# A decoder layer: four z tiles and most gate tiles computed ahead of the token mixers, the gate tiles in pairs by seven half-size products

## The chip, the cores and the metric

The kernel runs on one core of a Trainium2 chip. The metric is device time in microseconds (us), the median of three runs. PE is the matrix engine, PEld its weight loads, DVE the vector engine, ACT the scalar engine, POOL the GpSimd engine, and SP issues most DMA transfers.

## The reference

One layer of a decoder over 512 tokens and 2048 channels, all in float32: a token mixer, a cross-attention into 256 memory tokens, a feed-forward block with a short convolution, and a final norm. The change lies in the mixer. One matrix `w_in` (2048 rows) gives all its projections, among them `z` (1024 columns) and the logits of three gates (3 x 2048 columns):

```python
proj = xn @ w_in
dn_qkv, dn_z, dn_a, dn_b, swa_q, swa_kv, sb_qkv, gates = split_cols(proj, IN_SIZES)
...
o_dn = rmsnorm(o_dn, dn_norm) * silu(dn_z)
gate = sigmoid(gates).reshape(bsz, seq, 3, 2048)
merged = gate[:, :, 0] * (y_dn @ w_br_dn) + gate[:, :, 1] * (y_swa @ w_br_swa) + gate[:, :, 2] * (y_sb @ w_br_sb)
return merged @ w_o
```

`y_dn` comes from a recurrence over chunks (gated DeltaNet), `y_swa` from windowed attention, `y_sb` from stick-breaking attention.

## The kernel before

Activations lie feature-major: a tile is 128 features by 512 tokens. To keep float32 accuracy with the fast matrix format, every operand is split into a rounded part (`hi`, or `wh` of a weight) and the rest (`lo`, `wl`). `dense` (line 138) makes one tile of 128 output columns: for each of the 16 slices k of 128 input rows it issues three matmuls of 512 columns (lines 153 to 155: hi·wh, lo·wh, hi·wl), 48 in all. The weights come by SP in pieces of 1024 rows x 128 columns (512 KB, tile `raw`, three buffers); ACT rounds four slices at a time into `wh` (line 149), DVE subtracts to get `wl` (line 150), and each has four buffers of four slices. While PE works on some slices, ACT and DVE prepare the next.

The stages in order of the program: start (lines 164 to 281: norms, keys and values of the memory, matmuls of 256 columns since there are 256 memory tokens; x split into `hi`, `lo`); DeltaNet (lines 294 to 547: q, k, v of two heads at a time, then a long chain of small operations, between which the dense tiles of the next pair, and at the end the eight `z` tiles, stand on PE); the two attentions (lines 553 to 689, with their own dense tiles between small operations); gates and merge (lines 691 to 715); then `w_o`, cross-attention and feed-forward.

In the merge each of 16 column tiles m has, for each of three branches, one dense gate tile (48 matmuls, line 698), a sigmoid on ACT into `sg` (line 700), then a branch product of 24, 12 or 12 matmuls (line 707), a multiply by `sg` on DVE (710, 713) and a sum on POOL (714).

The order on each engine is made by a scheduler from data dependencies, buffers and priorities (weight loads and splits are given a high one); each engine then runs its list strictly in order and waits on semaphores.

Of the kernel before, what the change touches and what calls it, by code (L numbers as in the profile page):

```python
# [9 lines left out]
F32 = mybir.dt.float32  # L10
# [7 lines left out]
P = 128  # L18
# [40 lines left out]
def decoder_kernel(ctx: ExitStack, tc: tile.TileContext, x, mem, norm_mix, w_in, dn_conv, dn_a_log, dn_dt_bias, dn_norm,  # L59
# [13 lines left out]
    wsp = ctx.enter_context(tc.tile_pool(name="wsp", bufs=4))  # L73
    misc = ctx.enter_context(tc.tile_pool(name="misc", bufs=2))
    psd = ctx.enter_context(tc.tile_pool(name="psd", bufs=2, space=bass.MemoryType.PSUM))
    psum = ctx.enter_context(ExitStack())
    gen = []

# [41 lines left out]
    lo = [None] * KT  # L120

    def split_slot(k):
        hi[k] = main.tile([P, S], F32R, name=f"hi{k}")
        lo[k] = main.tile([P, S], F32R, name=f"lo{k}")
        return hi[k], lo[k]

    def mrg_tile(k):
        return main.tile([P, S], F32, name=f"mrg{k}")
# [9 lines left out]
    def dense(acc, w, r0, nk, col, hs, ls, M=P, share=False):  # L138
        for c0 in range(0, nk, 8):
# [3 lines left out]
            with tc.high_priority(1000000):  # L143
                nc.sync.dma_start(out=raw[:, :kc, :], in_=w[r:r + kc * P, col:col + M].rearrange("(k p) c -> p k c", p=P))
            for s0 in range(0, kc, 4):
                wh = wsp.tile([P, 4, M], F32R, name="wh")
                wl = wsp.tile([P, 4, M], F32R, name="wl")
                with tc.high_priority(1000000):
                    act.copy(wh, raw[:, s0:s0 + 4, :])  # L149
                    (pool if share and s0 else dve).tensor_tensor(wl, raw[:, s0:s0 + 4, :], wh.bitcast(F32), op=ALU.subtract)  # L150
                for j in range(4):
                    k = c0 + s0 + j
# [21 lines left out]
    with region("p_start") as ps:  # L174
        memT = [main.tile([P, S], F32R, name=f"mrg{k}") for k in range(KT)]
# [108 lines left out]

    def conv_silu(dst, acc, c):
# [8 lines left out]
    gen_pool("psg_dn", 3)  # L294
    y = [None] * 16
    with region("p_dn") as dp:
# [90 lines left out]
        for h0 in range(0, DNH, 2):  # L387
# [10 lines left out]
            # decays  # L398
# [15 lines left out]
            # keys  # L414
# [17 lines left out]
            # inverse of the unit lower triangular matrices, transposed: blocks of 8 by substitution, then doubling  # L432
# [40 lines left out]
            # queries and values  # L473
# [15 lines left out]
            # the recurrence over chunks  # L489
# [36 lines left out]
            # output norm  # L526
# [14 lines left out]
        for h in range(DNH):  # L541
            acc = dense_ps()
            dense(acc, w_in, 0, KT, O_Z + h * P, xh, xl)
            sz = misc.tile([P, S], F32, name="m0")
            last = act.activation(sz, acc, AF.Silu)
# [401 lines left out]
```

## Time and profile before

| | |
|---|---|
| median of 3 runs | 2918.39 us (2917.04 to 2918.99) |
| profiled execution: span from first to last instruction | 2917.2 us |
| PE busy | 2867.7 us, 98% |
| PEld, DVE, ACT, POOL busy | 81%, 45%, 36%, 9% |
| mean granted clock of PE | 0.996 |
| read from memory | 266.41 MB, 93 GB/s |

The profile comes from one execution; its span is its own time. Matmuls overlap, so the mean duration of one (392 ns for 512 columns) is not what the next one waits; that is read from start to start. Below, "L153" is line 153 of the kernel before.

### The profile page before, as it was taken

To read this page: it belongs to the slowest core of one execution; us is meant where nothing else is said; L and a number is where in the kernel's file an instruction comes from. 1 tells how busy PE (TensorE), PEld (TensorE's weight loads), DVE (VectorE), ACT (ScalarE), POOL (GpSimd) and SP (SyncE) were. 2 spreads that over 40 slices of the span, in tenths; PEclk is the share of its full clock that TensorE was granted. 3 is DMA by queue.
4 is the path that set the end of the run, shared out by engine and by line. 5 is a ranking of instruction groups with operands and counts; after the bars stand their busy time and mean duration, and the time that the engine had idled before them with its cause. 6 is when DMAs were issued, how large, how long until landed. Compare 5 with 4: busy or idle time off the path is not lost.

```text
span 2917.2 us, 34620 instructions
## 1 busy us (share of the span) xinstructions
PE 2867.7 (98%) x13463; PEld 2365.3 (81%) x13463; DVE 1322.4 (45%) x2305; ACT 1046.6 (36%) x1926; POOL 260.0 (9%) x195
## 2 busy tenths in 40 slices
PE   7999999999999999999999999999999999999998
PEld 7787887877778888888888887788888888888887
DVE  7466576336334223223224344544344434443445
ACT  6444344334443222222224334533223323322333
POOL 2100010100000000000000110201001000000002
PEclk9999999999999999999999999999999999999999
DMA  6322212232223333333334432333333333333333
GB/s 206 103 65 73 56 53 73 64 86 65 73 76 98 94 98 98 94 98 98 94 98 124 118 97 73 91 97 99 95 101 94 99 97 94 101 94 96 99 94 116
DMA packets 469941, 272.84 MB, mean 94 GB/s; under 512 B 11249, under 2 KB 450018, under 8 KB 469138
## 3 DMA queue, kind: packets, MB, share of 16 engines
q1 hardware_dynamic: 468576, 268.60, 32.4%
q8 instruction: 105, 1.72, 0.2%
q0 software_dynamic: 560, 1.79, 0.2%
q14 instruction: 58, 0.48, 0.0%
q10 hardware_dynamic: 642, 0.26, 0.0%
HBM read 266.41 MB, written 4.19 MB: 93 GB/s over the span
## 4 chain that ended last, share of the span: by engine, by line
PE 88%; DVE 3%; ACT 1%; issue 1%; POOL 1%; ACTq 0%; DVEq 0%; POOLq 0%
PE acc L155 21%; PE acc L153 21%; PE acc L154 21%; PE gps L875 4%; PE gps L873 4%; PE gps L874 4%; PE gps L153 2%; PE gps L155 2%; PE gps L154 2%; PE gps L471 1%; PE gps L466 1%; DVE wl L150 1%; PE gps L593 0%; PE gps L686 0%; PE gps L651 0%
## 5 line engine op out<-in xcount | busy, mean ns | idle before, releaser
L153 PE MATMUL acc<-hi,wh 128*128 128x512 f32 x2912 | 1140.8, 392 | 0.7 <-ACT hi L132 0.7
L154 PE MATMUL acc<-lo,wh 128*128 128x512 f32 x2912 | 1141.2, 392 | 0.0
L155 PE MATMUL acc<-hi,wl 128*128 128x512 f32 x2912 | 1141.2, 392 | 0.0
L150 DVE TENSOR_TENSOR wl<-raw,wh 128x512 fp32r<-128x512 f32 x826 | 589.0, 714 | 940.5 <-ACT wh L149 917.9
L149 ACT CAST wh<-raw 128x512 fp32r<-128x512 f32 x840 | 521.7, 622 | 1304.7 <-PE acc L154 1093.0
L155 PEld LDWEIGHTS acc<-hi,wl 128*128 128x128 f32 x2912 | 547.9, 188 | 113.0 <-issue 2.3
L153 PEld LDWEIGHTS acc<-hi,wh 128*128 128x128 f32 x2912 | 547.6, 188 | 113.3 <-issue 1.6
L154 PEld LDWEIGHTS acc<-lo,wh 128*128 128x128 f32 x2912 | 547.8, 188 | 111.6 <-issue 0.9
L868 DVE TENSOR_TENSOR wl<-raw,wh 128x512 fp32r<-128x512 f32 x112 | 77.7, 694 | 165.2 <-ACT wh L867 145.0
L867 ACT CAST wh<-raw 128x512 fp32r<-128x512 f32 x112 | 69.8, 623 | 206.7 <-PE gps L874 171.9
L875 PE MATMUL gps<-wl,mrg 128*128 128x512 f32 x368 | 143.3, 389 | 0.0
L873 PE MATMUL gps<-wh,mrg 128*128 128x512 f32 x368 | 143.2, 389 | 0.0
L874 PE MATMUL gps<-wh,mrg 128*128 128x512 f32 x368 | 143.2, 389 | 0.0
L847 POOL TENSOR_TENSOR u<-u 128x512 f32<-128x512 f32 x32 | 58.3, 1823 | 900.8 <-ACT wh L149 801.2
L714 POOL TENSOR_TENSOR mrg<-mrg,m 128x512 f32<-128x512 f32 x32 | 52.2, 1632 | 641.9 <-DVE m L713 641.9
L843 DVE SCALAR_TENSOR_TENSOR u<-v,ffcw,u 128x511 f32<-128x511 f32 (+1 forms) x128 | 96.1, 751 | 14.6 <-ACT u L839 12.3
L153 PE MATMUL gps<-yh,wh 128*128 128x512 f32 x256 | 99.8, 390 | 0.0
L155 PE MATMUL gps<-yh,wl 128*128 128x512 f32 x256 | 99.7, 389 | 0.0
L154 PE MATMUL gps<-yl,wh 128*128 128x512 f32 x256 | 99.7, 389 | 0.0
L837 DVE TENSOR_TENSOR v<-acc,rstd 128x512 f32<-128x512 f32 x64 | 44.3, 692 | 100.5 <-PE acc L155 100.5
L875 PEld LDWEIGHTS gps<-wl,mrg 128*128 128x128 f32 x368 | 69.1, 188 | 14.4
L874 PEld LDWEIGHTS gps<-wh,mrg 128*128 128x128 f32 x368 | 69.1, 188 | 14.3
(425 smaller groups left out, 2537.0 us busy)
## 6 DMA issues: line engine op xcount, KB each, us to landing
raw<-in_w_in_dram SPq DMA_DIRECT2D x196, 512.0 KB, 3.8
raw<-in_w_up_dram SPq DMA_DIRECT2D x128, 512.0 KB, 4.0
raw<-in_w_down_dram SPq DMA_DIRECT2D x64, 512.0 KB, 3.8
raw<-in_w_o_dram SPq DMA_DIRECT2D x32, 512.0 KB, 4.1
raw<-in_w_xkv_dram SPq DMA_DIRECT2D x16, 512.0 KB, 5.0
raw<-in_w_br_dn_dram SPq DMA_DIRECT2D x16, 512.0 KB, 4.0
xraw<-in_x_dram SPq DMA_DIRECT2D x4, 1024.0 KB, 9.3
raw<-in_w_br_swa_dram SPq DMA_DIRECT2D x16, 256.0 KB, 2.7
```

What stands on the lines that cost most here:

```text
L149: act.copy(wh, raw[:, s0:s0 + 4, :])
L150: (pool if share and s0 else dve).tensor_tensor(wl, raw[:, s0:s0 + 4, :], wh.bitcast(F32), op=ALU.subtract)
L153: pe.matmul(acc, wh[:, j, :], hs[k], start=(k == 0), stop=False)
L154: pe.matmul(acc, wh[:, j, :], ls[k], start=False, stop=False)
L155: pe.matmul(acc, wl[:, j, :], hs[k], start=False, stop=(k == nk - 1))
L843: dve.scalar_tensor_tensor(u[:, sh:S], v[:, 0:S - sh], w, u[:, sh:S], op0=ALU.mult, op1=ALU.add)
L847: pool.tensor_tensor(res[0], res[0], res[1], op=ALU.mult)
L867: act.copy(wh, raw[:, i, :])
L868: dve.tensor_tensor(wl, raw[:, i, :], wh.bitcast(F32), op=ALU.subtract)
L873: pe.matmul(acc, ah[j][:, ts], wh, start=(k == 0), stop=False)
L874: pe.matmul(acc, al[j][:, ts], wh, start=False, stop=False)
L875: pe.matmul(acc, ah[j][:, ts], wl, start=False, stop=(k == 7))
```

## The change

Right after the start stage the new kernel computes four of the eight z tiles (`z_tile`) and writes them to DRAM through POOL's DMA queue. Meanwhile DVE and ACT build four combinations of blocks of x (`sums`, tiles `fb`). Then the gate logits of the column tiles m = 2 to 15 are made in pairs, 21 pairs (7 pairs of m, three gates): rows in two halves of 1024, columns in two tiles of 128, tokens in two halves of 256. Each pair is a 2 x 2 by 2 x 2 block product and is made with seven block products (Strassen's scheme in Winograd's form). One product is eight slices, each with one matmul of 512 columns (wh against hi and lo of 256 tokens, side by side) and one of 256 columns (wl against hi). Sums of weight blocks (`combine`) and of results (`fold`) go to DVE; ACT copies two partial results from one PSUM accumulator into another as a start value (`act.copy(b, a)`, `act.copy(d, b)`). The pair's sigmoid goes to one buffer `g` and by POOL's DMA queue to DRAM. In the DeltaNet stage four z tiles are loaded by SP in place of being computed, and in the merge 42 of 48 gate tiles are. The weight buffers `wh`, `wl` are two of eight slices in place of four of four, in every `dense`. The memory region for the merged tiles is closed and opened again around the new stage.

```diff
--- before.py
+++ after.py
-    wsp = ctx.enter_context(tc.tile_pool(name="wsp", bufs=4))
+    wsp = ctx.enter_context(tc.tile_pool(name="wsp", bufs=2))
     misc = ctx.enter_context(tc.tile_pool(name="misc", bufs=2))
-    psd = ctx.enter_context(tc.tile_pool(name="psd", bufs=2, space=bass.MemoryType.PSUM))
+    dram = ctx.enter_context(tc.tile_pool(name="dram", bufs=1, space=bass.MemoryType.DRAM))
...
+    def open_std(n):
+        nonlocal mrgp, psd
+        psum.close()
+        std.close()
+        mrgp = std.enter_context(tc.tile_pool(name=f"mrgp{n}", bufs=1, reuse_waits="tile"))
+        psd = std.enter_context(tc.tile_pool(name=f"psd{n}", bufs=2, space=bass.MemoryType.PSUM, reuse_waits="tile"))
+    open_std(0)
...
-        hi[k] = main.tile([P, S], F32R, name=f"hi{k}")
-        lo[k] = main.tile([P, S], F32R, name=f"lo{k}")
+        both = main.tile([P, 2, S], F32R, name=f"x{k}")
+        hi[k], lo[k] = both[:, 0, :], both[:, 1, :]
+        xb[k] = both
         return hi[k], lo[k]
...
+            wh = wsp.tile([P, 8, M], F32R, name="wh")
+            wl = wsp.tile([P, 8, M], F32R, name="wl")
             for s0 in range(0, kc, 4):
-                wh = wsp.tile([P, 4, M], F32R, name="wh")
-                wl = wsp.tile([P, 4, M], F32R, name="wl")
+                part = slice(s0, s0 + 4)
                 with tc.high_priority(1000000):
-                    act.copy(wh, raw[:, s0:s0 + 4, :])
-                    (pool if share and s0 else dve).tensor_tensor(wl, raw[:, s0:s0 + 4, :], wh.bitcast(F32), op=ALU.subtract)
-                for j in range(4):
-                    k = c0 + s0 + j
+                    act.copy(wh[:, part, :], raw[:, part, :])
+                    (pool if share and s0 else dve).tensor_tensor(wl[:, part, :], raw[:, part, :], wh[:, part, :].bitcast(F32),
+                                                                  op=ALU.subtract)
+                for j in range(s0, s0 + 4):
+                    k = c0 + j
...
+    def z_tile(h):
+        acc = dense_ps()
+        dense(acc, w_in, 0, KT, O_Z + h * P, xh, xl)
+        sz = misc.tile([P, S], F32, name="m0")
+        return sz, act.activation(sz, acc, AF.Silu)
+    ZE = 4
+    HT = S // 2
+    MP = 2
+    z_d = [None] * ZE
+    gate_d = [[None] * KT for _ in range(3)]
+    psum.close()
+    std.close()
+    gp = std.enter_context(region("p_gate"))
+    psd = psum.enter_context(tc.tile_pool(name="psd_z", bufs=2, space=bass.MemoryType.PSUM, reuse_waits="tile"))
+    fb = [gp.tile([P, 2, 4, HT], F32R, name=f"fb{k}", bufs=1) for k in range(8)]
+    def sums(k):
+        u = gp.tile([P, 2, S], F32, name="sm")
+        for j in range(2):
+            dve.tensor_tensor(u[:, j, :], xh[k + 8 * j].bitcast(F32), xl[k + 8 * j].bitcast(F32), op=ALU.add)
+        b11, b12, b21, b22 = (u[:, j, t * HT:(t + 1) * HT] for j in range(2) for t in range(2))
+        v = gp.tile([P, 4, HT], F32, name="sm")
+        for i, (p_, q_) in enumerate(((b12, b11), (b22, v[:, 0, :]), (b22, b12), (b21, v[:, 1, :]))):
+            dve.tensor_tensor(v[:, i, :], p_, q_, op=ALU.subtract)
+        act.copy(fb[k][:, 0, :, :], v)
+        dve.tensor_tensor(fb[k][:, 1, :, :], v, fb[k][:, 0, :, :].bitcast(F32), op=ALU.subtract)
+    for h in range(ZE):
+        sz, _ = z_tile(h)
+        z_d[h] = dram.tile([P, S], F32, name=f"z{h}")
+        pool.dma_start(out=z_d[h], in_=sz)
+        for k in range(2 * h, 2 * h + 2):
+            sums(k)
+    psum.close()
+    with tc.tile_pool(name="psw", bufs=2, space=bass.MemoryType.PSUM, reuse_waits="tile") as pw:
+        banks = {n: [pw.tile([P, S], F32, name=n) for _ in range(2)] for n in ("sb", "sd")}
+        for n in ("sb", "sd"):
+            for t in banks[n]:
+                pe.matmul(t, xh[0][:, 0:P], xh[0], start=True, stop=True)
+        turn = [0]
+        def moving(form):
+            def of(k):
+                if form < 3:
+                    j, t = ((0, 0), (1, 0), (1, 1))[form]
+                    return xb[k + 8 * j][:, :, t * HT:(t + 1) * HT]
+                return fb[k][:, :, form - 3, :]
+            return of
+        B11, B21, B22, T1, T2, T3, T4 = (moving(i) for i in range(7))
+        def product(acc, w, of, first):
+            n = turn[0] = (turn[0] + 1) % 3
+            if n == 0:
+                wh, wl = (gp.tile([P, 8, P], F32R, name=f"s{n_}", bufs=1) for n_ in ("wh", "wl"))
+            else:
+                wh, wl = (wsp.tile([P, 8, P], F32R, name=n_) for n_ in ("wh", "wl"))
+            with tc.high_priority(1000000):
+                act.copy(wh, w)
+                dve.tensor_tensor(wl, w, wh.bitcast(F32), op=ALU.subtract)
+            av = acc.rearrange("p (h c) -> p h c", h=2)
+            for k in range(8):
+                m = of(k)
+                pe.matmul(av, wh[:, k, :], m, start=(first and k == 0), stop=False, skip_group_check=True)
+                pe.matmul(av[:, 0, :], wl[:, k, :], m[:, 0, :], start=False, stop=(k == 7), skip_group_check=True)
+        def fold(dst, half, other):
+            dve.tensor_tensor(dst, half, other, op=ALU.add)
+        def strassen_pair(w, col, out, straight):
+            quad = []
+            with tc.high_priority(1000000):
+                for i, (h, c) in enumerate(((0, 0), (1, 0), (0, 1), (1, 1))):
+                    r = rawp.tile([P, 8, P], F32, name="raw") if i % 2 else gp.tile([P, 8, P], F32, name="sraw", bufs=3)
+                    nc.sync.dma_start(out=r, in_=w[h * 8 * P:(h + 1) * 8 * P, col + c * P:col + (c + 1) * P]
+                                      .rearrange("(k p) c -> p k c", p=P))
+                    quad.append(r)
+            a11, a12, a21, a22 = quad
+            def combine(x_, y_, op):
+                s_ = gp.tile([P, 8, P], F32, name="sm")
+                with tc.high_priority(1000000):
+                    dve.tensor_tensor(s_, x_, y_, op=op)
+                return s_
+            a, b, c, d = (pw.tile([P, S], F32, name=n) for n in ("sa", "sb", "sc", "sd"))
+            product(a, a11, B11, True)
+            act.copy(b, a)
+            if straight:
+                product(a, a12, B21, False)
+            product(c, combine(a11, a21, ALU.subtract), T3, True)
+            s1 = combine(a21, a22, ALU.add)
+            s2 = combine(s1, a11, ALU.subtract)
+            s7 = misc.tile([P, S], F32, name="sg")
+            act.copy(s7, c)
+            product(b, s2, T2, False)
+            if not straight:
+                product(a, a12, B21, False)
+            act.copy(d, b)
+            la = misc.tile([P, HT], F32, name="m0")
+            act.copy(la, a[:, HT:S])
+            fold(out[:, 0, 0:HT], a[:, 0:HT], la)
+            s4 = combine(a12, s2, ALU.subtract)
+            product(d, s1, T1, False)
+            t = misc.tile([P, S], F32, name="m0")
+            dve.tensor_tensor(t, d, s7, op=ALU.add)
+            fold(out[:, 1, HT:S], t[:, 0:HT], t[:, HT:S])
+            product(b, a22, T4, False)
+            t = misc.tile([P, S], F32, name="m0")
+            dve.tensor_tensor(t, b, s7, op=ALU.add)
+            fold(out[:, 1, 0:HT], t[:, 0:HT], t[:, HT:S])
+            product(d, s4, B22, False)
+            la = misc.tile([P, HT], F32, name="m0")
+            act.copy(la, d[:, HT:S])
+            fold(out[:, 0, HT:S], d[:, 0:HT], la)
+        for m in range(MP, KT, 2):
+            for b_ in range(3):
+                g = gp.tile([P, 2, S], F32, name="g", bufs=1)
+                strassen_pair(w_in, O_G + b_ * D + m * P, g, m == MP and b_ == 0)
+                act.activation(g, g, AF.Sigmoid)
+                gd = dram.tile([P, 2, S], F32, name=f"gate{b_}_{m}")
+                pool.dma_start(out=gd, in_=g)
+                gate_d[b_][m], gate_d[b_][m + 1] = gd[:, 0, :], gd[:, 1, :]
+    open_std(1)
...
-            acc = dense_ps()
-            dense(acc, w_in, 0, KT, O_Z + h * P, xh, xl)
-            sz = misc.tile([P, S], F32, name="m0")
-            last = act.activation(sz, acc, AF.Silu)
+            if h < ZE:
+                sz = misc.tile([P, S], F32, name="sg")
+                nc.sync.dma_start(out=sz, in_=z_d[h])
+            else:
+                sz, last = z_tile(h)
             pool.tensor_tensor(y[h], y[h], sz, op=ALU.mult)
...
-                acc = dense_ps()
-                dense(acc, w_in, 0, KT, O_G + b * D + m * P, xh, xl)
                 sg = misc.tile([P, S], F32, name="sg")
-                last = act.activation(sg, acc, AF.Sigmoid)
+                if m < MP:
+                    acc = dense_ps()
+                    dense(acc, w_in, 0, KT, O_G + b * D + m * P, xh, xl)
+                    last = act.activation(sg, acc, AF.Sigmoid)
+                else:
+                    nc.sync.dma_start(out=sg, in_=gate_d[b][m])
                 if m == 0:
...
-                        wh = wsp.tile([P, S], F32R, name="wh")
-                        wl = wsp.tile([P, S], F32R, name="wl")
+                        if i == 0:
+                            whs, wls = (wsp.tile([P, 2, S], F32R, name=n) for n in ("wh", "wl"))
+                        wh, wl = whs[:, i, :], wls[:, i, :]
```

PE in the merge before (`gps` is the accumulator of a branch product, `acc` that of a gate tile, `yh`, `yl` the branch output, `hi`, `lo` the split x; the numbers are buffers). The end of one branch product and the beginning of the next gate tile:

```order
L153 MATMUL gps_8130<-yh11_7228,wh_8133 128x512
L154 MATMUL gps_8130<-yl11_7229,wh_8133 128x512
L155 MATMUL gps_8130<-yh11_7228,wl_8134 128x512
L153 MATMUL acc_8152<-hi0_497,wh_8155 128x512
L154 MATMUL acc_8152<-lo0_498,wh_8155 128x512
L155 MATMUL acc_8152<-hi0_497,wl_8156 128x512
```

PE at the like place now (column tile 3, from the first branch to the second):

```order
L168 MATMUL gps_11385<-yh7_10769,wh_11388 128x512
L169 MATMUL gps_11385<-yl7_10770,wh_11388 128x512
L170 MATMUL gps_11385<-yh7_10769,wl_11389 128x512
L168 MATMUL gps_11422<-yh8_10875,wh_11425 128x512
L169 MATMUL gps_11422<-yl8_10876,wh_11425 128x512
L170 MATMUL gps_11422<-yh8_10875,wl_11426 128x512
```

The 48 matmuls of a gate tile between two branch products are gone for column tiles 2 to 15.

PE in the new stage, between two block products of a pair (`sc`, `sb`: accumulators; `fb6`, `fb7`, `fb0`: combinations of x; `wh`, `wl`, `swh`, `swl`: split weights):

```order
L367 MATMUL sc_2469<-fb6_1008,wh_2494 128x512
L368 MATMUL sc_2469<-fb6_1008,wl_2495 128x256
L367 MATMUL sc_2469<-fb7_1009,wh_2494 128x512
L368 MATMUL sc_2469<-fb7_1009,wl_2495 128x256
L367 MATMUL sb_2468<-fb0_1002,swh_2520 128x512
L368 MATMUL sb_2468<-fb0_1002,swl_2521 128x256
L367 MATMUL sb_2468<-fb1_1003,swh_2520 128x512
L368 MATMUL sb_2468<-fb1_1003,swl_2521 128x256
```

Sixteen matmuls, half of them of 256 columns, stand here for each block product, 112 for each pair, where 96 of 512 columns stood.

ACT in the merge before, around one sigmoid (`sg<-acc`), and below it ACT in the new stage over one pair, from the rounding of the pair's second weight block (`raw_1921`) to that of the next pair's third product (`sm_2156`):

```order
L149 CAST wh_7545<-raw_7543 128x512
L149 CAST wh_7567<-raw_7565 128x512
L149 CAST wh_7583<-raw_7565 128x512
L149 CAST wh_7601<-raw_7599 128x512
L700 ACTIVATE sg_7540<-acc_7471 128x512
L149 CAST wh_7617<-raw_7599 128x512
```

```order
L362 CAST wh_2000<-raw_1921 128x1024
L391 COPY sb_1928<-sa_1927 128x512
L362 CAST wh_2026<-sm_1974 128x1024
L398 COPY sg_1978<-sc_1929 128x512
L362 CAST swh_2049<-raw_1925 128x1024
L402 COPY sd_1930<-sb_1928 128x512
L362 CAST wh_2072<-sm_2024 128x1024
L404 COPY m0_2021<-sa_1927 128x256
L362 CAST wh_2111<-sraw_2099 128x1024
L362 CAST swh_2134<-sm_2132 128x1024
L417 COPY m0_2092<-sd_1930 128x256
L362 CAST wh_2160<-sm_2156 128x1024
```

The start values `sb<-sa` and `sd<-sb`, which PE waits for, stand behind roundings of weights that themselves wait for PE to free a buffer.

## Rows read from the trace of the kernel before

**Rows 1.** Page, first line and part 1: busy time, share of the span, instructions.
```profile
span 2917.2 us, 34620 instructions
PE 2867.7 (98%) x13463; PEld 2365.3 (81%) x13463; DVE 1322.4 (45%) x2305; ACT 1046.6 (36%) x1926; POOL 260.0 (9%) x195
```
**Rows 2.** Page, part 4: the chain that ended last, by engine.
```profile
PE 88%; DVE 3%; ACT 1%; issue 1%; POOL 1%; ACTq 0%; DVEq 0%; POOLq 0%
```
**Rows 3.** Stretches: length, busy (instructions) PE, PEld, DVE, ACT, POOL; clock, DMA share, GB/s.
```profile
438.00:511.00 73.00, 67.86 (x343) 55.91 (x341) 49.62 (x115) 31.55 (x72) 6.24 (x5) 1.00 0.26 73
855.00:1520.00 665.00, 664.16 (x2932) 548.93 (x2931) 209.82 (x313) 193.19 (x316) 52.10 (x34) 1.00 0.35 96
```
**Rows 4.** Waits of PE: waiter, what for; us in total, times, longest.
```profile
PE gps L444 <- DVE xm L441: 10.3, 4, 3.3
PE gps L185 <- DMA rows_m<-in_norm_mem_dram: 6.1, 1, 6.1
PE acc L153 <- ACT hi L132: 0.7, 1, 0.7
```
**Rows 5.** ACT in the merge, in order of time: start us, us, line, tiles, [idle before].
```profile
904.41 0.62 ACT L149 CAST wh<-raw 128x512 fp32r<-128x512 f32 x1 [1.60 <-PE gps L154]
907.13 0.62 ACT L149 CAST wh<-raw 128x512 fp32r<-128x512 f32 x1 [2.10 <-PE acc L154]
909.85 0.62 ACT L149 CAST wh<-raw 128x512 fp32r<-128x512 f32 x1 [2.10 <-PE acc L154]
```
**Rows 6.** PE in the key and value projections, in order of time.
```profile
45.75 0.28 PE L153 MATMUL acc<-mrg,wh 128*128 128x256 f32 x1
45.87 0.28 PE L154 MATMUL acc<-mrg,wh 128*128 128x256 f32 x1
...
51.14 0.28 PE L154 MATMUL acc<-mrg,wh 128*128 128x256 f32 x1
```
**Rows 7.** PE groups by line: count | busy us, mean ns | idle before.
```profile
L155 PE MATMUL acc<-hi,wl 128*128 128x512 f32 x2912 | 1141.2, 392 | 0.0
...
L155 PEld LDWEIGHTS acc<-hi,wl 128*128 128x128 f32 x2912 | 547.9, 188 | 113.0 <-issue 2.3
```
**Rows 8.** DVE groups, shapes kept apart.
```profile
L150 DVE TENSOR_TENSOR wl<-raw,wh 128x512 fp32r<-128x512 f32 x826 | 589.0, 714 | 940.5 <-ACT wh L149 917.9 <-PE gps L874 6.1 <-PE gps L640 6.1
...
L508 DVE COPY vn<-gps 128x256 f32<-128x256 f32 x16 | 6.8, 423 | 5.2 <-PE gps L506 5.2
...
L439 DVE TENSOR_TENSOR am<-e,bl 128x1024 f32<-128x1024 f32 x4 | 4.9, 1218 | 0.1
```
**Rows 9.** DVE without idle time, in order of time.
```profile
344.14 0.69 DVE L150 TENSOR_TENSOR wl<-raw,wh 128x512 fp32r<-128x512 f32 x1
344.74 1.22 DVE L533 TENSOR_TENSOR kd<-gps,st 128x1024 f32<-128x1024 f32 x1
345.87 1.52 DVE L290 SCALAR_TENSOR_TENSOR qT<-acc,dncw,qT 128x511 f32<-128x511 f32 x2
```
**Rows 10.** ACT groups, shapes kept apart.
```profile
L468 ACT COPY am<-gps 128x512 f32<-128x512 f32 x32 | 17.2, 589 | 39.8 <-PE gps L466 39.8
...
L132 ACT CAST sph<-ssp 128x1152 fp32r<-128x1152 f32 x4 | 4.6, 1159 | 4.2 <-DVE ssp L658 4.2
...
L412 ACT ACTIVATE e<-e 128x1024 f32<-128x1024 f32 x4 | 4.2, 1062 | 0.9 <-DVE e L409 0.9
```
**Rows 11.** DMA issues: tiles, queue, count, KB each, median us to landing.
```profile
raw<-in_w_in_dram SPq DMA_DIRECT2D x196, 512.0 KB, 3.8
...
raw<-in_w_xkv_dram SPq DMA_DIRECT2D x16, 512.0 KB, 5.0
...
gfb<-in_norm_final_dram POOLq DMA_DIRECT2D x1, 1024.0 KB, 5.4
...
sink<-in_swa_sinks_dram POOLq DMA_DIRECT2D x1, 4.0 KB, 6.6
```
**Rows 12.** DVE while POOL runs beside it, in order of time.
```profile
74.69 2.33 DVE L150 TENSOR_TENSOR wl<-raw,wh 128x512 fp32r<-128x512 f32 x1 [1.95 <-ACT wh L149]
```

More of the change, by code (lines that the diff above doesn't have):

```diff
@@ L72, in decoder_kernel @@
     rawp = ctx.enter_context(tc.tile_pool(name="rawp", bufs=3))
-    wsp = ctx.enter_context(tc.tile_pool(name="wsp", bufs=4))
+    wsp = ctx.enter_context(tc.tile_pool(name="wsp", bufs=2))
     misc = ctx.enter_context(tc.tile_pool(name="misc", bufs=2))
-    psd = ctx.enter_context(tc.tile_pool(name="psd", bufs=2, space=bass.MemoryType.PSUM))
+    dram = ctx.enter_context(tc.tile_pool(name="dram", bufs=1, space=bass.MemoryType.DRAM))
+    std = ctx.enter_context(ExitStack())
     psum = ctx.enter_context(ExitStack())
     gen = []
+    mrgp = psd = None
+    def open_std(n):
[5 more added lines that the diff above has]
+    open_std(0)
     def gen_pool(name, bufs):
@@ L120, in decoder_kernel @@
     lo = [None] * KT
+    xb = [None] * KT
     def split_slot(k):
-        hi[k] = main.tile([P, S], F32R, name=f"hi{k}")
-        lo[k] = main.tile([P, S], F32R, name=f"lo{k}")
+        both = main.tile([P, 2, S], F32R, name=f"x{k}")
+        hi[k], lo[k] = both[:, 0, :], both[:, 1, :]
+        xb[k] = both
         return hi[k], lo[k]
     def mrg_tile(k):
-        return main.tile([P, S], F32, name=f"mrg{k}")
+        return mrgp.tile([P, S], F32, name=f"mrg{k}")
     def split(h, l, src, gain=None):
@@ L174, in decoder_kernel @@
     with region("p_start") as ps:
-        memT = [main.tile([P, S], F32R, name=f"mrg{k}") for k in range(KT)]
+        memT = [mrgp.tile([P, S], F32R, name=f"mrg{k}") for k in range(KT)]
         memraw = [ps.tile([P, D], F32, name="memraw", bufs=2) for _ in range(2)]
@@ L848, in up_pair @@
             n = j % 10
-            where, tags = (main, (f"mrg{2 * n}", f"mrg{2 * n + 1}")) if n < 8 else (gp, (f"ah{n}", f"al{n}"))
+            where, tags = (mrgp, (f"mrg{2 * n}", f"mrg{2 * n + 1}")) if n < 8 else (gp, (f"ah{n}", f"al{n}"))
             ah[j] = where.tile([P, S], F32R, name=tags[0], bufs=1)
```

## The prediction

> **What bounds the kernel now.** First the page's busy times [rows 1]: the reader is to see PE at 98% of the span and every other engine under half. Next the chain that ended last [rows 2]: 88% of it is PE itself. Then the stretches [rows 3]: in the merge, where the gate tiles stand, PE is busy 664.16 of 665.00 us while DVE and ACT work less than a third; in the DeltaNet stage it misses about 5 us in 73. Last PE's own waits [rows 4], which are a few microseconds each. So a removed matmul is worth its pitch on PE, provided that nothing else becomes late.
>
> The pitch is read from start to start, since durations overlap. In the merge ACT is released once per four slices, that is every 12 matmuls, at 904.41, 907.13 and 909.85 us [rows 5]: 2.72 us / 12 = 226.7 ns for a matmul of 512 columns (its duration reads 392 [rows 7]). Matmuls of 256 columns stand in the projections of the memory: the starts from 45.75 to 51.14 us are 46 [rows 6], 5.39 / 45 = 119.8 ns. Each has its own weight load; its 188 ns [rows 7] are hidden there under neighbours of 119.8 ns. Half the columns thus cost 53%, not 50%: 13 ns of every pitch do not shrink with the columns.
>
> **The change, part by part.** *Gate matmuls.* Removed are 42 gate tiles of 48 matmuls, for a pair 96 x 226.7 = 21.76 us. Added for a pair are 7 products x 8 slices x (226.7 + 119.8) ns = 19.40 us. The difference is 2.36 us, times 21 pairs: **-49.6 us**. The columns alone (43,008 in place of 49,152) would promise an eighth, 2.72 us a pair; the sixteen extra fixed parts take the rest. No row of before shows a moving operand that lies in two pieces of 256 columns, nor the two shapes in turn. Bounds: no cost, or one more fixed part of 13 ns for each of the 1176 long matmuls, +15.4 us. I take none, since a piece is as long as the whole operand of the nearest rows [rows 6].
>
> The Trainium skill gives another pitch (TensorE: Matmul & The Clock Gate, section "Back-to-back issue gap"): columns / 2.4 GHz + 2.5 ns, so 215.8 and 109.2 ns. By it the saving would be 21 x (20.72 - 18.20) = 52.9 us. The rows are 11 ns above it at both widths, and the rows decide.
>
> *Preparation in the new stage.* For a pair DVE has 7 subtractions and 4 weight sums of 1024 columns, 2 sums of 512 and 4 folds of 256. From rows: 11 x 1.22 (L439), 2 x 0.69, 4 x 0.42 (L508) = 16.5 us [rows 8]; from start to start it is less, since 512 take 0.60 and 1024 take 1.13 us without idle time [rows 9]: some 15 us. ACT has 7 roundings of 1024, 3 copies of 512, 2 of 256 and the sigmoid: 7 x 1.06 + 3 x 0.59 + 2 x 0.4 + 1.06 = 11.1 us [rows 10] (a 1152-wide rounding takes 1.16). Both lie beside PE's 19.40. Sums do not exclude a wait in order, so I walk through one pair. A product takes 2.77 us; three weight buffers rotate, so ACT may round for a product when the third one before it ends, 5.5 us ahead of need; rounding and subtraction take 1.1 + 1.2 us. In ACT's list the start value sb<-sa comes behind the rounding of the second block: product one ends at 2.8 us, the rounding ends at 3.9, the copy at 4.5; PE needs it at 5.5. The copy sd<-sb comes behind the rounding of a22 likewise: 8.3, 9.4, 10.0, needed at 11.1. At the seam of two pairs the sigmoid stands ahead of the next pair's rounding and copy, and 0.9 us remain. On DVE the addition that empties sd ends 1 us before PE writes sd again. I take 0 for waits; the margins are 0.9 to 1.2 us.
>
> *Ahead of the pairs.* Four z tiles are moved, not added: 192 matmuls here and 192 fewer in DeltaNet. Beside their 43.5 us on PE, DVE makes eight times 2 x 0.69 + 4 x 0.42 + 1.22 = 4.28 us of combinations and 16 weight subtractions of 0.69: 45.3 us by durations, about 39.5 from start to start. Between 0 and +6; I take +1. Four matmuls that set up accumulators: +0.9.
>
> *Handovers.* Memory and accumulators change hands before z, before the pairs and before DeltaNet. The nearest row, the turn from merge to w_o, costs PE 0.7 us [rows 4]; I take +2 for all, with +6 as the upper bound. That same 0.7 may go, since the splits for w_o can now be made during the merge.
>
> *Weight buffers of eight slices everywhere.* A buffer comes free after 24 matmuls where it was 12, so preparation is at least 5.4 us ahead where it was 8.2. Where DVE is blocked by the DeltaNet chain (its longest PE wait is 3.3 us [rows 4]) this may show: bounds 0 and +8 (a third more of the idle time that DeltaNet has), I take +3.
>
> *Merge without gates.* For a column tile PE has 48 branch matmuls, 10.9 us; SP loads 1 MB of weights and three gate tiles of 256 KB. Loads of 512 KB land in 3.8 us, 5.0 when crowded [rows 11]. With two sg buffers a gate load is issued when the multiply two products back is done and is needed after two products, at least 5.4 us later; the weight loads behind it on SP have three buffers in hand. Hidden; if SP's queue slipped by a whole product, 14 x 2.7 = 38 us would be the price.
>
> The sum is -49.6 + 0.9 + 1 + 2 + 3 = -42.7, on the profiled span of 2917.2: 2874.5. The median of the runs lies 1.2 above that span; so **2876 us**, 1.5% less.
>
> **The rivals.** *A, the split operand costs* (or the short matmuls do not hide the load before a long one): -42.7 + 15.4 = -27.3, 2891. For it: no row shows the form. Against it: rows 6.
>
> *B, ACT is late with start values: slower.* Place: sb<-sa and sd<-sb, twice a pair. Their list position behind a rounding that waits for a PE buffer makes PE wait for ACT and ACT for PE. If each rounding and copy stands bare, 1.06 + 0.59 + 0.1 for the signals = 1.75 us, x 42 = 73.5: 2876 + 73.5, about 2949. It decides from about 1.0 us of lateness of ACT (the margin) and passes the old time at 2.0 us in each of the 42. Against it: ACT is at 57% by the sum above.
>
> *C, gates written late: slower.* There is one buffer g; its write starts about 3 us into the next pair, and the first fold of that pair stands on DVE at about 13 us, ahead of weight subtractions. POOL's own transfers land in 5.4 to 6.6 us [rows 11]; from 11 us on DVE waits and PE after it. A landing of 15 us would cost 4 x 20 = 80 us: 2956. The rows also show that DVE and POOL hold each other up: a subtraction of 0.69 took 2.33 us beside POOL's work [rows 12]. The Trainium skill's "SBUF — State Buffer", section "SBUF: two separate sides", speaks for C: DVE work on the port it shares with GpSimd keeps POOL from writing its transfer descriptors, and the transfer waits. By that rule a write would wait for at most the DVE instruction in progress, 1.2 us, within the margin; but DVE is now busy most of the stage.
>
> *D, small waits add up* in DVE's list (handovers, eight-slice buffers, weight blocks that land late) to within a few us of the old time: about 2915.
>
> **How the numbers follow.** Forecast 0.66 (its own range 2864 to 2886), A 0.14, B 0.09, C 0.05, D 0.06. The range holds 8 in 10 when it takes the forecast, A and some of the partial forms of B and D: 2864 to 2908. Its lower end is -49.6 with no other term and a few us less waiting in DeltaNet. The measurement tells 0.2%, 5.8 us, from no change. Faster: the forecast, A and part of D, 0.82; same: most of the rest of D, 0.04; slower: B and C, 0.14.
>
> **What would show it.** Right: in the pairs a pitch of 346 to 347 ns from one long matmul to the next, 19.4 to 19.6 us for a pair, PE busy throughout; in the merge 10.9 us for a column tile. Wrong in the price: a pitch near 360 ns with PE without idle time (A). Wrong in the cover: waits of PE for L391 or L402 (B), of DVE at L371 for a transfer from g (C), of PE for L363 spread over the stage (D). In DeltaNet the idle time of PE should grow by a few us and no more.

## Result and the profile after

The changed kernel takes 2885.23 us (2884.96 to 2886.30, four executions) where the kernel before took 2918.47: the ratio is 0.9888, with a 95% interval of 0.9874 to 0.9902. The forecast was 2876 in a range of 2864 to 2908. The saving is 33 us where 42.7 were worked out, and most of the document from here on is about those 9 us.

The page's first line and part 1 of the kernel after, to be held against [rows 1]:

```profile
span 2883.5 us, 35374 instructions
PE 2826.4 (98%) x13803; PEld 2341.0 (81%) x13803; DVE 1543.9 (54%) x2550; ACT 1107.7 (38%) x1996; POOL 260.3 (9%) x220
```

PE is still busy 98% of the span, DVE has 221 us more to do. Stretches of the kernel after (columns as in [rows 3]): four z tiles, the 21 pairs, DeltaNet with the first attention's dense tiles, the merge, the output projection of the cross-attention:

```profile
83.45:129.30 45.85, 44.63 (x198) 36.64 (x198) 44.85 (x75) 21.79 (x30) 2.04 (x4) 1.00 0.51 137
129.30:547.30 418.00, 416.37 (x2354) 360.29 (x2353) 323.29 (x353) 213.75 (x271) 10.87 (x21) 1.00 0.45 128
547.30:1043.70 496.40, 486.32 (x2637) 404.21 (x2635) 297.07 (x641) 199.29 (x467) 51.44 (x45) 1.00 0.26 72
1291.70:1516.70 225.00, 225.00 (x993) 186.24 (x993) 118.65 (x160) 68.99 (x118) 48.88 (x31) 1.00 0.48 144
1775.10:1831.00 55.90, 50.72 (x241) 38.56 (x239) 31.18 (x45) 35.34 (x61) 19.64 (x15) 1.00 0.31 88
```

and the last of them in the kernel before:

```profile
1815.80:1866.00 50.20, 49.09 (x239) 38.49 (x238) 30.67 (x44) 34.17 (x60) 21.79 (x15) 1.00 0.32 93
```

In the merge PE has no idle time left at all. In the pairs it has next to none either, but they take 418 us where 407.4 were worked out. The output projection of the cross-attention, which the change seems not to touch, is 5.7 us longer. The waits of PE (waiter, what for; total, times, longest), for [rows 4]:

```profile
PE gps L590 <- DVE xm L587: 7.0, 4, 2.0
PE acc L168 <- ACT wh L163: 5.1, 8, 1.2
PE gps L971 <- DVE mrg L965: 4.5, 5, 1.8
...
PE sd L367 <- ACT sd L402: 1.5, 1, 1.5
```

DeltaNet's wait (L444 before, now L590) has become shorter, 7.0 for 10.3 us. Those at L168 and L971 have grown, from 1.0 and 0.3 us, and stand mostly in the cross-attention. The start values cost one wait in the first pair and no more.

One product in the kernel after, in order of time (start, duration, line, operation):

```profile
304.21 0.40 PE L367 MATMUL sb<-fb,wh 128*128 128x512 f32 x1
304.44 0.28 PE L368 MATMUL sb<-fb,wl 128*128 128x256 f32 x1
304.56 0.40 PE L367 MATMUL sb<-fb,wh 128*128 128x512 f32 x1
...
307.04 0.40 PE L367 MATMUL sd<-x,swh 128*128 128x512 f32 x1
```

Eight slices take 2.83 us. Over the 962 slices that start between 160 and 500 us a short matmul starts 236.2 ns after its long one and the next long one 117.1 ns after that, read from the trace's whole nanoseconds: 353.3 ns a slice in place of 346.5, the same in products on x and on the stored combinations. A pair takes 19.79 us.

The account by terms. A saving is negative; counts of matmuls are those of the program.

| term | forecast | profile after | profile of e6 |
|---|---|---|---|
| gate matmuls: 1176 slices, less 42 x 48 x 226.7 ns = 457.0 | -49.6 | -41.5 | -49.3 |
| waits and restarts in the pairs | 0 | +2.3 | +2.6 |
| z ahead of the pairs and set-up (46.05 for 43.5) | +1.9 | +2.5 | +2.6 |
| handovers, start stage | +2 | -0.8 | -1.5 |
| DeltaNet and attention | +3 | -2.4 | -2.4 |
| cross-attention and feed-forward | 0 | +6.4 | +6.4 |
| sum | -42.7 | -33.5 | -41.6 |
| span less 2917.2 | | -33.7 | -41.8 |

DeltaNet and attention run from the stage's first matmul to the first branch product, 794.2 us before and 744.4 after, with 209 dense matmuls fewer: 192 of z and 17 of a gate tile that stood there. 209 x 0.2267 = 47.4, so 2.4 us of waiting are gone. In the merge there are 1999 matmuls fewer and 453 us less, which is their pitch and nothing else.

### The profile page after: what moved, and what is told of

Same layout as the page of the kernel before. It is cut to its first block, busy times and chain, and to the rows that moved or that the text cites. A ratio compares the mean times of both kernels' runs of the same rounds, so it can differ in the third digit from the quotient of the medians.

```text
span 2883.5 us, 35374 instructions
## 1 busy us (share of the span) xinstructions
PE 2826.4 (98%) x13803; PEld 2341.0 (81%) x13803; DVE 1543.9 (54%) x2550; ACT 1107.7 (38%) x1996; POOL 260.3 (9%) x220
## 4 chain that ended last, share of the span: by engine, by line
PE 70%; DVE 4%; ACT 2%; issue 1%; POOL 1%; ACTq 0%; POOLq 0%; DVEq 0%
PE acc L168 15%; PE acc L169 15%; PE acc L170 15%; PE gps L1026 4%; PE gps L1024 4%; PE gps L1025 4%; PE gps L168 2%; PE gps L169 2%; PE gps L170 2%; PE gps L612 1%; PE gps L617 1%; DVE wl L164 1%; PE gps L740 0%; ACT wh L163 0%; ACT junk L674 0%
## 5 line engine op out<-in xcount | busy, mean ns | idle before, releaser
L168 PE MATMUL acc<-x,wh 128*128 128x512 f32 x2240 | 879.0, 392 | 3.3 <-ACT wh L163 2.6
L169 PE MATMUL acc<-x,wh 128*128 128x512 f32 x2240 | 879.5, 393 | 0.0
L170 PE MATMUL acc<-x,wl 128*128 128x512 f32 x2240 | 878.2, 392 | 0.0
L163 ACT CAST wh<-raw 128x512 fp32r<-128x512 f32 x672 | 385.8, 619 | 803.5 <-PE acc L169 561.8
L164 DVE TENSOR_TENSOR wl<-raw,wh 128x512 fp32r<-128x512 f32 x658 | 463.8, 743 | 415.3 <-ACT wh L163 414.8
L168 PEld LDWEIGHTS acc<-x,wh 128*128 128x128 f32 x2240 | 421.1, 188 | 90.8 <-ACT wh L163 4.7
L170 PEld LDWEIGHTS acc<-x,wl 128*128 128x128 f32 x2240 | 421.1, 188 | 87.7 <-issue 2.3
L169 PEld LDWEIGHTS acc<-x,wh 128*128 128x128 f32 x2240 | 421.2, 188 | 85.7 <-issue 1.8
L1019 DVE TENSOR_TENSOR wl<-raw,wh 128x512 fp32r<-128x512 f32 x112 | 72.4, 688 | 144.3 <-ACT wh L1018 144.3
L1018 ACT CAST wh<-raw 128x512 fp32r<-128x512 f32 x112 | 63.9, 619 | 202.1 <-PE gps L1025 175.6
L997 POOL TENSOR_TENSOR u<-u 128x512 f32<-128x512 f32 x32 | 41.3, 1290 | 919.3 <-DVE u L993 919.3
L168 PE MATMUL gps<-yh,wh 128*128 128x512 f32 x256 | 99.7, 389 | 0.0
L363 DVE TENSOR_TENSOR wl<-sm,wh 128x1024 fp32r<-128x1024 f32 x56 | 68.6, 1226 | 51.8 <-ACT wh L362 51.8
L362 ACT CAST wh<-sm 128x1024 fp32r<-128x1024 f32 x56 | 58.8, 1050 | 71.0 <-PE sb L367 23.8
L367 PE MATMUL sb<-fb,wh 128*128 128x512 f32 x232 | 83.5, 399 | 0.1
```

What stands on the lines that cost most here:

```text
L163: act.copy(wh[:, part, :], raw[:, part, :])
L164: (pool if share and s0 else dve).tensor_tensor(wl[:, part, :], raw[:, part, :], wh[:, part, :].bitcast(F32), op=ALU.subtract)
L168: pe.matmul(acc, wh[:, j, :], hs[k], start=(k == 0), stop=False)
L169: pe.matmul(acc, wh[:, j, :], ls[k], start=False, stop=False)
L170: pe.matmul(acc, wl[:, j, :], hs[k], start=False, stop=(k == nk - 1))
L363: dve.tensor_tensor(wl, w, wh.bitcast(F32), op=ALU.subtract)
```

## The experiments

The first two, timed with the next two on one chip, asked why a slice takes 353.3 ns: theory S, the moving operand in two pieces; theory T, the turn between the two lengths.

**e1: combinations of x in one piece.**
```diff
-    fb = [gp.tile([P, 2, 4, HT], F32R, name=f"fb{k}", bufs=1) for k in range(8)]
+    fb = [gp.tile([P, 4, 2, HT], F32R, name=f"fb{k}", bufs=1) for k in range(8)]
...
-                return fb[k][:, :, form - 3, :]
+                return fb[k][:, form - 3, :, :]
```


> The four combinations of x are stored so that the rounded part and the rest of one combination lie side by side: the moving operand of four of the seven products is then one piece of 512 columns; that of the three products on x itself stays in two pieces. Theory S (a moving operand in two pieces costs about 7 ns for each long matmul and the short one behind it): long-to-long pitch 346 to 347 ns in the products with fb, 353.4 as before in those with x; 672 x 6.9 ns = 4.6 us less, 2880.6 us. Theory T (the turn between a long and a short matmul costs it): 353.4 ns everywhere, 2885.2 us.


Measured: 2878.19 us, ratio 0.9872 (0.9859 to 0.9886); three executions from 2877.0 to 2879.0 and one at 2884.9. In the profile a slice takes 346.6 ns with the combinations, and 346.6 too with x, whose operand was still in two pieces. S foretold the first and not the second, T neither.

**e2: eight long matmuls, then eight short ones.**
```diff
                 pe.matmul(av, wh[:, k, :], m, start=(first and k == 0), stop=False, skip_group_check=True)
+            for k in range(8):
+                m = of(k)
                 pe.matmul(av[:, 0, :], wl[:, k, :], m[:, 0, :], start=False, stop=(k == 7), skip_group_check=True)
```


> Within a product all eight long matmuls come first, then the eight short ones; operands as in the changed kernel. Theory T (the turn costs): long pitch 226.7 ns, short pitch 119.8 ns, 346.5 ns a slice, 1176 x 6.9 = 8.1 us less, 2877.1 us. Theory S (two pieces cost): long pitch stays near 236.7 ns, short pitch 119.8, so 356.5 a slice or 3.6 us more, 2885 to 2889 us.


Measured: 2880.58 us (2878.8 to 2881.8), 0.9875 (0.9862 to 0.9889), between the two. By itself it settled nothing.

**e3: the weight buffers alone.** The kernel before, with `wsp` as two buffers of eight slices.
```diff
-    wsp = ctx.enter_context(tc.tile_pool(name="wsp", bufs=4))
+    wsp = ctx.enter_context(tc.tile_pool(name="wsp", bufs=2))
...
+            wh = wsp.tile([P, 8, M], F32R, name="wh")
...
-                wh = wsp.tile([P, 4, M], F32R, name="wh")
...
```


> The kernel before with one part of the change alone: weight buffers wh, wl two of eight slices in place of four of four, in every dense and in the last stage. Theory W (a dense over four slices fills only half of such a buffer, so the output projection of the cross-attention has two buffers in rotation where it had four): the stretch of that projection (50.2 us before) grows by 5 to 6 us with waits of PE for the transposed sums and for ACT's rounding, the rest stays, 2921 to 2925 us. Rival (the loss there comes from another part of the change, such as the new place of the split x): that stretch stays at 50 us, 2918 us. My forecast's own term (the buffers cost 3 us in DeltaNet): idle time of PE in DeltaNet grows.


Measured: 2918.76 us, 1.0008 (0.9999 to 1.0016). Waits of PE in this kernel:

```profile
PE gps L446 <- DVE xm L443: 6.9, 4, 1.9
...
PE acc L155 <- ACT wh L150: 5.0, 8, 1.0
PE gps L823 <- DVE mrg L817: 4.5, 5, 1.8
```

These are the three rows of the kernel after, to a tenth of a microsecond, and the stretch from the cross-attention to the last matmul is longer by the same 6.4 us (5.7 of them in the output projection, 55.5 for 49.8 us). So both belong to the buffers: the loss in the cross-attention (W), and the shorter wait in DeltaNet, where the forecast had put their cost. The time of the whole stays within 2 us because one, with a shorter start stage (80.3 us in this profile, 84.2 before), nearly pays for the other. How much of that start is due to the buffers is not shown: PE's granted clock from 35 to 63 us was 0.82 in the profile before and 1.00 in this one.

**e5: the gate tiles early, but plain.** In the place of the products each gate tile is a `dense` of 48 matmuls.
```diff
-            product(a, a11, B11, True)
...
+            for i, acc in enumerate((a, b)):
+                dense(acc, w, 0, KT, col + i * P, xh, xl)
+                act.activation(out[:, i, :], acc, AF.Sigmoid)
```


> The changed kernel with the 42 gate tiles in the same place, through DRAM as before, but each as a plain dense of 48 matmuls (no seven products, no four set-up matmuls; the combinations of x are still made). Theory (the products alone carry the gain, moving costs little): the stage takes 42 x 48 x 226.7 ns = 457 us where it took 417.8, 2885.2 + 38 = 2923 us, within 3. Rival (moving the work forward helps by itself, through DeltaNet or the merge): 2918 us or less.


Measured: 2922.02 us (2920.7 to 2923.7), 1.0017 (1.0008 to 1.0026). Moving the gates and four z tiles, with the buffers and the combinations, costs about 5 us; the seven products have to earn that first, and then the rest.

Then the changed kernel itself was run again, next to three variants on another chip.

**e6: the changed kernel again**, without an edit.


> The changed kernel as it is, beside the kernel before and the next three on one chip. In the runs so far products with x and with the stored combinations have one pitch, 353.4 ns in the changed kernel and 346.6 in both variants of it, though the operand on x was in two pieces in all of them: theories S and T, as put, both fail. Theory P (the seven nanoseconds belong to the chip or the placement of a run, not to operand layout or order): here 230.0 ns from long to short, 346.6 for both, about 2878 us. Theory L (layout of the combinations in memory sets the pitch of every long matmul): 236.7 and 353.4 again, 2885 us.


Measured: 2877.2, 2877.5, 2885.3 and 2886.7 us: two groups, 7.8 to 9.5 us apart, on one chip with one program (ratio 0.9878, 0.9861 to 0.9894). The profile is of the 2877.2:

```profile
304.09 0.39 PE L367 MATMUL sd<-x,swh 128*128 128x512 f32 x1
304.32 0.28 PE L368 MATMUL sd<-x,swl 128*128 128x256 f32 x1
304.44 0.39 PE L367 MATMUL sd<-x,swh 128*128 128x512 f32 x1
...
306.17 0.39 PE L367 MATMUL sa<-x,wh 128*128 128x512 f32 x1
```

Six slices take 2.08 us, 346.7 ns each, all through the stage. 1176 x 6.67 ns = 7.8 us, about the distance of the groups. The slower two have no profile; but the profile of this same program at 2885.28 us, under the result, has the longer pitch. So the pitch belongs to the execution; it is not the layout (L), nor the chip alone. The account of this execution is in the last column of the table.

**e7: shared buffers in the output projection.** Its sums run over four slices only, so each of two eight-slice buffers was half empty; now two column tiles share one.
```diff
...
-            dense(acc, w_xo, 0, 4, m * P, oh, ol)
+            if m % 2 == 0:
+                pair = [wsp.tile([P, 8, P], F32R, name=n) for n in ("wh", "wl")]
+            half = slice(4 * (m % 2), 4 * (m % 2) + 4)
+            dense(acc, w_xo, 0, 4, m * P, oh, ol, bufs=[t[:, half, :] for t in pair])
```


> The changed kernel, but in the output projection of the cross-attention (sums over four slices) two column tiles share one weight buffer of eight slices, so that four quarter sums are ahead again in place of two. Theory W: that stretch falls from 55.5 to about 50 us, 5 to 6 us less than the run of the changed kernel beside it. Rival (the wait there is for the sums on DVE, not for buffers): no change.


Measured: 2879.02 us (2878.4 to 2879.9), 0.9869 (0.9854 to 0.9883). The profile has 353.3 ns a slice, so it is to be held against the executions of e6 at 2885.3 and 2886.7: 5.5 to 8.3 us less. By stretches, from w_o's end to the last matmul, 5.7 us less than the profile of e6, and the wait of PE for the sums at DVE's `mrg` (4.5 us) has left the list. This is what the buffers cost there: in the kernel before, PE went from the transposes of one tile (L821) without idle time to the next matmuls,

```profile
1826.97 0.40 PE L153 MATMUL acc<-hi,wh 128*128 128x512 f32 x1
1827.22 0.66 PE L821 MATMUL gps<-ident,mrg 128*128 128x128 f32 x4
1827.63 0.47 PE L153 MATMUL gps<-hi,wh 128*128 128x512 f32 x1
```

and in the changed kernel, which had no split weights for the next tile yet, the transposes stand right behind the tile whose sum they need:

```profile
1788.25 0.39 PE L170 MATMUL acc<-x,wl 128*128 128x512 f32 x1
1789.42 0.66 PE L971 MATMUL gps<-ident,mrg 128*128 128x128 f32 x4 [0.78 <-DVE mrg L965]
1789.83 0.47 PE L168 MATMUL gps<-x,wh 128*128 128x512 f32 x1
```

**e8: the edits of e1 and e7 together.**


> Combinations of x in one piece and the shared buffers of the output projection together. Theory P: the same as the run with shared buffers alone, within 1 us. Theory L: 7 to 8 us less than that.


Measured: 2871.0 us once, 2878.6 to 2879.6 three times, 0.9862 (0.9847 to 0.9877). The profiled execution is one of the three:

```profile
304.08 0.40 PE L370 MATMUL sb<-fb,wh 128*128 128x512 f32 x1
...
306.56 0.40 PE L370 MATMUL sd<-x,swh 128*128 128x512 f32 x1
```

Seven slices in 2.48 us; the mean over the stage is 353.3 ns (236.4 and 117.0), with the combinations in one piece. The longer pitch comes with that layout too, so S falls for good.

**e9: all gates early.** e8 with the gates of column tiles 0 and 1 also in pairs.
```diff
-    MP = 2
+    MP = 0
```


> As the run before (one piece, shared buffers), and the gates of column tiles 0 and 1 go with the rest: three more pairs, no dense gate tile left in the merge. If a pair is worth what the other 21 are worth (21.76 - 19.41 = 2.35 us): 7.0 us less than the run before. Rival (those tiles were the filler of the second attention's waits and of the turn to the merge, which now stand bare): 0 to 5 us more than the run before.


Measured: 2888.80 us (2886.5 to 2891.3), 0.9900 (0.9884 to 0.9917): 10 us more than e8, where the rival had 0 to 5. The three pairs take 59.3 us more ahead, as they should, and the merge is 48.7 us shorter; but from the first matmul of attention scores to the first branch product the time stays at 248 us (248.1 in e8, 248.2 here) though 61 matmuls of gate tiles that PE did there, 13.8 us, are gone. The end of the second attention, two waits of PE and two stretches with the granted clock (third from the right):

```profile
PE gps L820 <- ACT sph L145: 7.0, 1, 7.0
...
PE gps L836 <- ACT sz L833: 2.0, 1, 2.0
```
```profile
1325.00:1337.00 12.00, 4.56 (x19) 2.69 (x17) 3.35 (x6) 6.95 (x10) 0.41 (x2) 0.84 0.16 48
1337.00:1351.00 14.00, 9.64 (x23) 6.36 (x23) 4.72 (x7) 4.29 (x7) 1.22 (x3) 0.50 0.01 1
```

Without the tile PE is busy 4.56 of 12 us, and then the granted clock falls to 0.50, the 1.2 GHz level: eight matmuls at L836 take 4.63 us, 2.32 in e7. In e7, with the tile, the like stretches (1265 to 1277, 1277 to 1291) have PE busy 12.00 and 12.30 us at a clock of 1.00. The gate tiles of the two column tiles were not left over; they cover the attention's end.

The last four asked what the longer pitch hangs on, and tested the walk through ACT's list. They ran on a third chip.

**e10: e7 again, as their measure.**


> The kernel with shared output buffers once more, as the measure for the next three on the same chip. In the runs so far executions of one kernel differ by 8 us, and the profiles have one of two pitches for a slice of a product, 346.7 or 353.3 ns, throughout the stage: executions near 2871 or near 2879 us are expected.


Measured: 2879.28 us (2879.1 to 2880.3), 0.9867 (0.9854 to 0.9881), profile 353.3 ns (236.4 and 116.9). The second group did not show here.

**e11: the edits of e2 and e7 together.**


> Shared output buffers, and in each product the eight long matmuls first, then the eight short ones. Theory T2 (each turn from short to long or back can cost one step of 6.7 ns, and the two pitches are that): with 2 turns a product in place of 16 the executions agree within 2 us and lie at 2873 to 2875 us. Theory U (each long matmul can cost it): two groups of executions 8 us apart remain.


Measured: 2873.92 us, five executions from 2873.2 to 2874.3, 0.9848 (0.9835 to 0.9862).

```profile
300.68 2.00 PE L370 MATMUL sb<-fb,wh 128*128 128x512 f32 x8
302.52 1.11 PE L373 MATMUL sb<-fb,wl 128*128 128x256 f32 x8
303.48 2.00 PE L370 MATMUL sd<-x,swh 128*128 128x512 f32 x8
```

A product takes 2.79 us over the stage, as it does in e2 on another chip, against 2.77 and 2.83 with the lengths in turn. The five executions form one group, within T2's range and at neither of the two places that U foretold, 2871 and 2879. That no second group showed says less, since e7 and e10 have all the turns and showed none in four executions each. Nor does T2's step stand at the turns: in the trace's nanoseconds the first short matmul starts 226.7 ns after the last long one, and the first long one 120.0 ns after the last short one, as in streams of one length. What a product has above such streams, 21 ns, is 27 ns in the starts behind the turn to the long ones (233, 236, 228, 233 and 231 ns apart, then 226.7) less 7 behind the turn back (113, 119, then 120.0). It is also the fastest kernel here that keeps its time.

**e12: all matmuls of a slice of 512 columns**, with e7's edit.
```diff
-                pe.matmul(av[:, 0, :], wl[:, k, :], m[:, 0, :], start=False, stop=(k == 7), skip_group_check=True)
+                pe.matmul(av, wl[:, k, :], m, start=False, stop=(k == 7), skip_group_check=True)
```


> Shared output buffers, and the second matmul of a slice takes both halves too, 512 columns like the first (it adds the product of the two rests); the two-piece operand on x and the stride of the combinations are as in the changed kernel. Theory T2: no turn, so every matmul has the 226.7 ns of a dense, 453.3 a slice, the stage is 1176 x 453.3 = 533 us and the time 2871 + 1176 x 106.6 ns = 2996 us with no second group of executions. Theory S (two pieces cost): a pitch over 230 ns, 3004 us and more.


Measured: 2995.85 us (2995.3 to 2997.2), 1.0267 (1.0253 to 1.0281).

```profile
300.45 0.39 PE L370 MATMUL sb<-fb,swh 128*128 128x512 f32 x1
300.68 0.39 PE L371 MATMUL sb<-fb,swl 128*128 128x512 f32 x1
...
304.08 0.39 PE L370 MATMUL sd<-x,wh 128*128 128x512 f32 x1
```

Sixteen matmuls take 3.63 us, 226.7 ns each, on operands in two pieces and with the same stride between combinations: rival A's price for a split operand is nothing. What is left is the turn, or what a short matmul does to the weight load of the long one behind it; e12 takes both away, and no run separates them.

**e13: start values late.** e7, and ahead of each copy of a start value five more copies on ACT.
```diff
...
+            for _ in range(5):
+                act.copy(junk, a[:, 0:HT])
             act.copy(b, a)
...
+            for _ in range(5):
+                act.copy(junk, b[:, 0:HT])
             act.copy(d, b)
```


> Shared output buffers, and ahead of each of the two copies of a start value ACT makes five extra copies of 256 columns (0.36 us each, results unused). In ACT's list the copy for sb now also stands behind one more rounding, which waits for PE. By the forecast's walk (margin 1.1 and 1.2 us) and the price of rival B: a wait of PE of about 1.75 us at sb and of 5 x 0.36 - 1.2 = 0.6 us at sd, 21 x 2.35 = 49 us more than the run with shared buffers, about 2925 us. If the margin were larger than the walk gives: less than 20 us more.


Measured: 2937.87 us (2935.8 to 2938.9), 1.0067 (1.0053 to 1.0080): 58.6 us more than e10, and slower than the kernel before. Waits of PE:

```profile
PE sb L370 <- ACT sb L397: 33.1, 20, 3.3
PE sd L370 <- ACT sd L410: 14.3, 20, 3.4
```

1.66 and 0.72 us a time (1.57 and 0.57 in the steady pairs), for 1.75 and 0.6 expected; the extra copies took 0.37 each. A steady pair takes 22.45 us where e10 has 19.79. Of these 2.66 us the two waits are 2.14; the other 0.52, some 11 us over the stage, is lost around the stops, where the product behind a stop takes about 0.1 us more. In the first two pairs, with a granted clock of 0.92 and 0.84, some 5 us more are lost. Rival B was a real danger, and the margins were about as wide as the forecast's walk had them.

## Why the prediction was right, and where it was off

*The pitch sets the worth of a removed matmul: right.* The merge lost 1999 matmuls and 453 us. e5 shows that the products alone carry the gain.

*The price of a slice, 346.5 ns: right in some executions, 6.7 ns short in others.* The profiles of the result and of e6 have one each. Rival A had named a dearer slice, at twice the size; e1, e8 and e12 refute its first reason, the split operand. Its second, that short matmuls do not hide the load before a long one, is not tested by itself. This is 8 of the 9 us. The step that failed is "the nearest rows": [rows 5] and [rows 6] are streams of one length, and no row of before showed the two in turn, as the forecast had said itself; its upper bound covered it.

*ACT in time with the start values: right.* The walk gave margins of 0.9 to 1.2 us; in the profile after the copy at the seam ends 1.10 us ahead of PE's start of sb at 315.52 (0.93 in e6, at the forecast's pitch),

```profile
313.84 0.58 ACT L391 COPY sb<-sa 128x512 f32<-128x512 f32 x1
```

and the one for sd 1.2 us ahead (1.16 in e6). e13 took the margin away and found the loss. In the first pair, which has no lead, PE waits 1.5 us; the whole +2.3, for which the forecast had 0, lies in the first two pairs (21.72 and 20.14 us).

*Gates written late (C): did not happen.* The next pair's first fold on DVE starts 10.2 us after the write is issued; the write has landed long before, and DVE never waits at L371 for it:

```profile
gate<-g POOLq DMA_DIRECT2D x21, 512.0 KB, 2.9
```

The forecast had weighed a rule of the Trainium skill for it (SBUF — State Buffer, "SBUF: two separate sides"), by which DVE's work on the port it shares keeps POOL from writing descriptors. DVE is busy 323 of 418 us in this stage, and the longest landing is 4.2 us against a median of 2.9, while POOL's issuing instruction takes 0.53 to 0.55 us all 21 times. Whether the rule acts in these 2.9 us no run here shows; if it does, the price lies within the margin.

*z ahead of the pairs: right.* +2.5 for +1.9, of which 1.2 us is the handover to the pairs (below), with DVE busy 44.85 of 45.85 us; this is the one stretch where DVE nearly bounds.

*Weight buffers of eight slices, +3 in DeltaNet: wrong place and sign there.* e3 has PE waiting 3.4 us less for DVE's `xm` in DeltaNet (some 2 us net, since other waits there grew) and 6.4 us more in and behind the cross-attention, with the buffers alone. The forecast counted slices ahead in a dense over sixteen slices and did not look for the dense that fills only half a buffer; e7 gives back 5.7 of the 6.4. D had named eight-slice buffers, for DVE's list in general, and not this place.

*Handovers, +2: right in size, though the table hides it.* Two waits of PE stand at them in the kernel after:

```profile
PE gps L236 <- ACT m L233: 1.7, 2, 1.4
...
PE sb L342 <- ACT m L305: 1.2, 1, 1.2
```

The 1.4 us of the first stand right ahead of z, where the kernel before has 0.8 us at the like place, between dense matmuls of DeltaNet; the second stands ahead of the pairs, and the table counts it with z. The turn to DeltaNet has none. The start stage as a whole is 0.8 us shorter, but its two profiles differ in the granted clock (third from the right), before and after:

```profile
35.00:63.00 28.00, 23.90 (x159) 23.23 (x160) 25.79 (x58) 16.89 (x28) 11.30 (x7) 0.82 0.42 117
35.00:63.00 28.00, 23.25 (x190) 22.20 (x189) 26.16 (x61) 18.81 (x32) 13.31 (x7) 1.00 0.43 119
```

So what the change did to the start is left open.

*How near the sum came is in part luck.* In the profile of e6, where the slice had its price, the account ends 1.1 us from the forecast, because 6.4 us lost in and behind the cross-attention and 2.6 in the first two pairs, for which the forecast had nothing, stand against 5.4 us better than forecast in DeltaNet and 3.5 in the start.

Open also: what decides in an execution which of the two pitches it has. That turns of length are needed for it is suggested by e11 and e12, with one group of executions each and a steady 226.7 ns in e12, but not shown, since e7 and e10 had one group too; that a turn as such costs a step is not shown either, since e6 makes the same turns without it.

## What to carry to other kernels

When a buffer is made larger and fewer, look for the users that fill only part of it: their depth falls with the count of buffers, and they may stand stages away from the change. A piece of plain work left among small dependent operations may be worth more there than the cheaper form of it elsewhere: look at what PE does beside it before taking it away. Where an ACT copy feeds PE, its margin in the list can be read from an order and a few durations, and is worth reading before anything is put ahead of it.

## What the hardware showed that was not expected

A matmul of 512 columns followed by one of 256 takes 346.7 ns in one execution and 353.3 in another of the same program, steadily through 400 us; the difference of 6.7 ns is 16 cycles at 2.4 GHz. At the shorter pitch every slice is alike, 230.0 + 116.7. At the longer one the slices go round in threes: in the kernel after, 641 of 962 take 349 or 350 ns and every third 360 or 361, on average 236.2 + 117.1, and e8 and e10 show the same round. Only the trace's whole nanoseconds show this, not the views, which print hundredths of a microsecond. The steady streams have 226.7 and 119.8.

In e9 the granted clock fell to the 1.2 GHz level after a stretch in which PE was busy 4.56 of 12 us, and was 0.91 in the next 15 us. The merge gave back 48.7 us for 227 matmuls fewer, which at 226.7 ns are 51.5.
